# Output projection of a hybrid attention/gMLP layer from normalised inputs: one PSUM accumulation per piece, with a shorter 1/sqrt and other ends

## The chip, the cores and the metric

The kernel runs on one core of a Trainium2 chip. The metric is the device time of one execution in microseconds, taken as the median over runs. All arithmetic is float32 in effect: each operand of a large matrix product is split into a high and a low part of the narrower type fp32r, and three matmuls (high by high, low by high, high by low) stand for one product.

## The reference

One layer on 1056 tokens of width 1024 (1024 prompt tokens and 8 samples of 4 tokens). Cut to what matters here:

```python
x = x + 0.5 * swiglu(rmsnorm(x, ffn1_norm))           # FFN 1, width 2816
h = rmsnorm(x, mix_norm) @ w_in                       # q, k, v, u, g
attn = sink_attention(q, k, v)                        # 512 channels, window 128
gate = gelu(u) * (tril(w_s) @ rmsnorm(gelu(g)) + b)   # 512 channels, chunks of 128
x = x + concat(rmsnorm(attn, attn_out_norm),
               rmsnorm(gate, gmlp_out_norm)) @ w_out  # the output projection
x = x + 0.5 * swiglu(rmsnorm(x, ffn2_norm))           # FFN 2
y = rmsnorm(x, final_norm)
```

The output projection contracts over 1024 channels: 512 from the attention ("which = 0") and 512 from the gate ("which = 1"). Each half has a normalisation of its own, so each has a factor r per token, 1/sqrt(mean square), and a gain per channel.

## The kernel before, in words

Tokens lie in the free dimension, channels in the 128 partitions. The tokens are worked in two halves h = 0, 1 of 528, and a half in two pieces of 264, so that a piece fits one PSUM bank. Stages follow each other: FFN 1 (to about 700 us), the mixer (about 700 to 1080 us), FFN 2 and the final norm. A tile framework schedules each engine's instructions ahead of time; on the chip every engine runs its own queue in order, and waits at its head.

**Mixer.** A list of jobs sets the order: 28 jobs of the input projection (`proj`, 48 matmuls each, PSUM tile `pp`), then 16 of the output projection (`out_proj`, tile `pw`). The attention blocks (scores `sc` L860, exponentials on ACT L869, the sink's exponential L871, division L876, transposes `ptr` L883, product `po` L889) and the gate's pieces (`spatial`: transposes `pt` L788, squares L814, norm `gn` L819, mix `pm` L835 to L841) are generators that an interleaver `I` lets in between the matmuls of the jobs, at a rate per stage. Each job's weight, 128x1024, is loaded, cast on ACT (`whi` L114) and its remainder is taken by DVE or POOL (`wlo` L115). The weight of the next job is asked for when a job begins.

**Output projection.** `split_out` waits until a half's raw outputs are there, applies the gain and splits (`ah` ACT L972, `al` DVE L973). `out_proj` makes, for each output block d of 128 channels, each piece and each of the two contraction halves apart, 12 matmuls into a bank of its own. DVE multiplies the bank by r (`wo` L984), POOL adds the product to the residual x (L986). r comes from `norm_out` and `rstd`: squares summed over channel tiles (`oacc` L176), a sum over partitions by matmul (`pn` L150), 1/sqrt by integer guess and three Newton steps of three DVE operations on 128x5 elements (`tiny_rsqrt` L136 to L141, tiles `gt`, `gr`, `gv`), and a broadcast by matmul (`pr` L165). After the second half of the contraction, `final` splits x for FFN 2 (`xh` ACT L193, `xl` DVE L194), adds its squares (`acc` L176, on POOL for h = 0) and stores x.

**Start.** Ten warm-up matmuls, then x and the first weight block arrive by DMA; ACT casts two quarters of the weight (`wb` L121) and then makes the first operand (`xh` L193).

**End.** The last output piece of FFN 2 (`pd` L620, added to x on DVE L572) gets its square on ACT (L172), the square is added to the sum on DVE (`facc` L176), `pn` sums over partitions, DVE makes 1/sqrt, `pr` broadcasts it, ACT copies it (L1085), DVE and POOL scale the eight channel tiles (L1092, L1090), and the result is stored.

Of the kernel before, what the change touches and what calls it, by code (L numbers as in the profile page):

```python
# [11 lines left out]
F32 = mybir.dt.float32  # L12
# [28 lines left out]
def build(nc, tc, ctx, A):  # L41
# [91 lines left out]
    def tiny_rsqrt(a, n):  # L133

        b, c = small("gr", 5)[:, :n], small("gt", 5)[:, :n]
        V.tensor_scalar(c.bitcast(I32), a.bitcast(I32), 1, None, op0=ALU.arith_shift_right)  # L136
        V.tensor_scalar(b.bitcast(I32), c.bitcast(I32), -1, 0x5F3759DF, op0=ALU.mult, op1=ALU.add)
        for i in range(3):
            V.tensor_mul(c, b, b)
            V.scalar_tensor_tensor(c, c, -0.5, a, op0=ALU.mult, op1=ALU.mult)  # L140
            V.scalar_tensor_tensor(a if i == 2 else b, c, 1.5, b, op0=ALU.add, op1=ALU.mult)  # L141

    def rstd(acc, o, n, mul, eps, put):

        full, rest = n // 128, n % 128
        nj = full + (rest > 0)
        p = pst("pn")
        for j in range(nj):
            m = min(128, n - j * 128)
            PE.matmul(p[:m, j:j + 1], lhsT=acc[:, o + j * 128:o + j * 128 + m], rhs=ones[:, 0:1], start=True, stop=True)  # L150
        v = small("gv", 5)
        if rest:
            V.memset(v, 1.0)
            V.tensor_scalar(v[:rest, full:nj], p[:rest, full:nj], mul, eps, op0=ALU.mult, op1=ALU.add)
        V.tensor_scalar(v[:, :full], p[:, :full], mul, eps, op0=ALU.mult, op1=ALU.add)
        tiny_rsqrt(v[:, :nj], nj)
        yield 0.3, LAT["rstd"]

        p = pst("pr")
        for j in range(nj):  # L160
            m = min(128, n - j * 128)
            if j == 4:
                put(p, o)
                p = pst("pr2")
            PE.matmul(p[:, j % 4 * 128:j % 4 * 128 + m], lhsT=v[:m, j:j + 1].to_broadcast([m, 128]), rhs=ident[:m, :m], start=True, stop=True)  # L165
        put(p[:, :n] if nj <= 4 else p[:, :rest], o if nj <= 4 else o + 512)
        yield 1.0, 1
# [475 lines left out]
    pw = pst("warm")  # L643
    for _ in range(10):
        PE.matmul(pw[:, :128], lhsT=ones, rhs=ones, start=True, stop=True)
# [3 lines left out]
    for k in range(4):  # L649
        P1.split(0, k)  # L650
# [193 lines left out]
    def attention(b):  # L844
# [102 lines left out]
    parts, done = [[None, None], [None, None]], set()  # L947
    orst, held = [[None, None], [None, None]], []
# [4 lines left out]
    def norm_out(h, which):  # L953
        src, _ = raw_out(h, which)
        n = T[h]
        acc, r = tmp("oacc"), tmp("orst")
        orst[h][which] = r
# [4 lines left out]
        done.add((h, which))  # L962

    def split_out(h, which):
        I.until(lambda: finished.get((h, which)) is True)
        src, g0 = raw_out(h, which)
        n = T[h]
        hi, lo = Quad(f"ah{which}", 4, F32R), Quad(f"al{which}", 4, F32R)
        parts[h][which] = hi, lo
        for k in range(4):  # L970
            x, g = src(k, 0, n), gains[:, g0 + k:g0 + k + 1]
            S.activation(hi(k, 0, n), x, AF.Copy, scale=g)  # L972
            V.scalar_tensor_tensor(lo(k, 0, n), x, g, hi(k, 0, n).bitcast(F32), op0=ALU.mult, op1=ALU.subtract)  # L973

    def out_proj(h, which, i, w, prep, rate):
        hi, lo = parts[h][which]
        for d in (2 * i, 2 * i + 1):
            for hh, o, n in HPIECES[h]:
                p = pst("pw")
                mm3(p, n, w, hi, lo, range(4), o, lambda k: (4 * (d % 2) + k) * 128)  # L980

                def evac(d=d, o=o, n=n, p=p):
                    t = tmp("wo")
                    V.tensor_mul(t[:, :n], p[:, :n], orst[h][which][:, o:o + n])  # L984
                    x = X[h](d, o, n)
                    G.tensor_add(x, x, t[:, :n])  # L986
                    if which == 0 and (h, o, n) == HPIECES[h][-1]:
                        prep(h, d)
                held.append(evac)
                I(n * 12 / 2400, rate)  # L990
                if len(held) > 4:
                    I.until(lambda: (h, which) in done)
                if (h, which) in done:
                    while held:
                        held.pop(0)()
# [24 lines left out]
    jobs = [("p", h, kind, i) for h in range(2) for kind, i in kinds] + [("o", h, which, i) for h in range(2) for which in (1, 0) for i in range(4)]  # L1020
# [8 lines left out]
    def weight(t, h, kind, i):  # L1029
        return wload(A["w_in"][{"k": 0, "v": 1, "q": 2, "u": 6, "g": 10}[kind] + i] if t == "p" else A["w_out"][kind, i], lo_on=G if t == "p" and i else None)  # L1030

    w = weight(*jobs[0])
    wnext = weight(*jobs[1])
    for k in range(8):
        Pm.square(1, k)
    for job, ahead in zip(jobs, jobs[1:] + [None]):
        if job != jobs[0]:
            wnext = weight(*ahead) if ahead else None
# [35 lines left out]
    def one(piece, h, o, n, d):  # L1074
# [3 lines left out]
        squares(fin[piece], X[h](d, o, n), 0, n, first, V if piece else G)  # L1078
# [18 lines left out]
        ends.append(rstd(fin[piece], 0, n, 1.0 / D, 1e-6, put))  # L1097
# [39 lines left out]
def layout(i):  # L1137
# [11 lines left out]
    a["w_out"] = np.concatenate([w[:512][hd], w[512:]]).reshape(2, 4, 128, 4, 2, 128).transpose(0, 3, 2, 4, 1, 5).reshape(2, 4, 128, 1024)  # L1149
# [51 lines left out]
```

## Time and profile before

| | |
|---|---|
| time, three runs | 1785.37, 1787.62, 1787.37 us; median 1787.37 us |
| profiled execution | 1785.29 us, of which the span is 1783.5 us |
| TensorE busy | 1741.6 us of the span |
| VectorE busy | 1221.6 us |
| ScalarE busy | 730.9 us |
| GpSimd busy | 158.4 us |
| mean granted TensorE clock | 0.989 of full |

PE is TensorE's matmul, DVE is VectorE, ACT ScalarE, POOL GpSimd; L984 is line 984 of the kernel. A row of the timeline gives start, duration, engine, line, operation, output and inputs, and in square brackets how long the engine had been idle before and which engine's instruction ended that. A row of groups gives the total and the mean of one, and the idle time before them. Matmuls are pipelined: a 128x264 matmul is shown with a duration of 0.28 us, but the next one starts about 0.12 us later.

### The profile page before, as it was taken

Reading aid. Unit: us, or ns where it says so; the run is one execution under the profiler, and the core shown is the slowest. Engines: PE = TensorE matmul, PEld = TensorE weight load, DVE = VectorE, ACT = ScalarE, POOL = GpSimd, SP = SyncE. Lnnn points to the kernel's source line nnn. Section 1 sums busy time; section 2 is a strip of 40 time slices with the busy share of each in tenths; the row PEclk is TensorE's granted clock in tenths of the full one; section 3 lists DMA queues with packets and bytes.
Section 4 is the critical chain, followed back from the end, with each engine's and each line's share of the span. In section 5 each row is a group of like instructions: output and inputs, shape, how many; then the busy total and the mean of one; then the engine's idle time right before and its main releaser. Section 6 shows DMA issues by size and latency. Waiting matters only on the chain.

```text
span 1783.5 us, 34092 instructions
## 1 busy us (share of the span) xinstructions
PE 1741.6 (98%) x14045; PEld 1713.3 (96%) x14045; DVE 1221.6 (68%) x2151; ACT 730.9 (41%) x1288; POOL 158.4 (9%) x140
## 2 busy tenths in 40 slices
PE   9999999999999999999997899999999999999997
PEld 9999999999999999988977899999999999999997
DVE  7986766666556755488677886986666666457566
ACT  6533333333343444255464434633333333344341
POOL 0000000000000011221211571000000000000110
PEclk9999999999999999999998999999999999999998
DMA  6054544454495544112222232254544454586532
GB/s 240 28 190 160 201 157 150 145 201 150 153 378 169 166 135 140 67 49 75 72 72 65 101 102 85 67 206 149 195 153 140 172 182 138 209 327 200 175 107 98
DMA packets 104460, 266.05 MB, mean 149 GB/s; under 512 B 12384, under 2 KB 15136, under 8 KB 104288
## 3 DMA queue, kind: packets, MB, share of 16 engines
q1 hardware_dynamic: 104304, 263.87, 43.1%
q8 instruction: 110, 1.80, 0.4%
q14 instruction: 46, 0.38, 0.1%
HBM read 190.25 MB, written 74.60 MB: 148 GB/s over the span
## 4 chain that ended last, share of the span: by engine, by line
PE 79%; DVE 11%; issue 6%; POOL 2%; ACT 2%; DMA 0%; POOLq 0%; SPq 0%; DVEq 0%; ACTq 0%
PE pa L430 24%; PE pd L620 22%; PE pc L430 12%; PE pp L130 7%; PE pb L430 6%; PE pg L396 4%; PE pw L130 2%; POOL x L986 2%; DVE tl L299 1%; DVE wb L122 1%; ACT P L869 1%; DVE P L876 1%; DVE P L865 1%; PE po L889 1%; DVE raw L269 1%
## 5 line engine op out<-in xcount | busy, mean ns | idle before, releaser
L430 PE MATMUL pa<-th,wb 128*128 128x264 f32 x2624 | 494.7, 285 | 1.1 <-DVE wb L122 0.6
L430 PEld LDWEIGHTS pa<-th,wb 128*128 128x128 f32 x2624 | 413.1, 189 | 2.3 <-DVE wb L122 0.9
L430 PE MATMUL pa<-tl,wb 128*128 128x264 f32 x1312 | 374.3, 285 | 2.9 <-DVE tl L299 2.9
L620 PE MATMUL pd<-hh,whi 128*128 128x264 f32 x1208 | 343.9, 285 | 0.0
L620 PE MATMUL pd<-hl,whi 128*128 128x264 f32 x1208 | 343.8, 285 | 0.0
L620 PE MATMUL pd<-hh,wlo 128*128 128x264 f32 x1208 | 343.8, 285 | 0.0
L121 ACT CAST wb<-raw 128x512 fp32r<-128x512 f32 x296 | 181.3, 620 | 279.2 <-PE pc L430 83.4
L122 DVE TENSOR_TENSOR wb<-raw,wb 128x512 fp32r<-128x512 f32 x296 | 204.4, 700 | 107.1 <-ACT wb L121 106.5
L430 PEld LDWEIGHTS pa<-tl,wb 128*128 128x128 f32 x1312 | 247.6, 189 | 3.3 <-DVE tl L299 3.3
L430 PE MATMUL pc<-th,wb 128*128 128x264 f32 x1280 | 247.4, 285 | 1.4 <-DVE x L468 0.9
L620 PEld LDWEIGHTS pd<-hh,wlo 128*128 128x128 f32 x1208 | 227.6, 188 | 0.0
L620 PEld LDWEIGHTS pd<-hh,whi 128*128 128x128 f32 x1208 | 227.5, 188 | 0.1
L620 PEld LDWEIGHTS pd<-hl,whi 128*128 128x128 f32 x1208 | 227.3, 188 | 0.0
L430 PEld LDWEIGHTS pc<-th,wb 128*128 128x128 f32 x1280 | 204.0, 189 | 2.1 <-DVE x L468 1.1
L367 DVE TENSOR_TENSOR wlo<-raw,whi 128x1024 fp32r<-128x1024 f32 x82 | 94.8, 1156 | 134.7 <-ACT whi L366 125.9
L430 PE MATMUL pc<-tl,wb 128*128 128x264 f32 x640 | 182.6, 285 | 0.0
L269 DVE TENSOR_TENSOR raw<-raw 128x512 f32<-128x512 f32 x248 | 169.3, 691 | 16.0 <-DMA raw<-f_d 11.1
L366 ACT CAST whi<-raw 128x1024 fp32r<-128x1024 f32 x82 | 79.9, 980 | 216.1 <-PE pd L620 146.6
L130 PE MATMUL pp<-xh,wlo 128*128 128x264 f32 x448 | 129.3, 289 | 4.0 <-POOL wlo L115 4.0
L130 PE MATMUL pp<-xh,whi 128*128 128x264 f32 x448 | 131.7, 294 | 0.7 <-ACT whi L114 0.3
L130 PE MATMUL pp<-xl,whi 128*128 128x264 f32 x448 | 128.5, 287 | 0.0
L430 PEld LDWEIGHTS pc<-tl,wb 128*128 128x128 f32 x640 | 120.5, 188 | 0.3 <-DVE tl L299 0.3
(233 smaller groups left out, 3016.3 us busy)
## 6 DMA issues: line engine op xcount, KB each, us to landing
raw<-f_gu SPq DMA_DIRECT2D x86, 512.0 KB, 4.2
raw<-f_d SPq DMA_DIRECT2D x74, 512.0 KB, 3.9
ws_s<-raw SPq DMA_DIRECT2D x88, 256.0 KB, 2.0
ht<-ht_s SPq DMA_DIRECT2D x40, 528.0 KB, 7.6
raw<-ws_s SPq DMA_DIRECT2D x40, 512.0 KB, 8.4
raw<-w_in SPq DMA_DIRECT2D x28, 512.0 KB, 4.3
ht_s<-m SPq DMA_DIRECT2D x44, 264.0 KB, 2.2
ht<-ht SPq DMA_DIRECT2D x20, 528.0 KB, 3.8
```

The lines of the kernel that those rows point to most:

```text
L121: S.copy(w[:, 0], src)
L122: V.tensor_sub(w[:, 1], src, w[:, 0].bitcast(F32))
L130: PE.matmul(p[:, :n], lhsT=w[a][:, c:c + 128], rhs=b(k, o, n), start=(3 * i + j == 0), stop=(3 * i + j == last))
L269: V.tensor_add(b[dst], b[dst], b[x])
L299: V.tensor_sub(lo, src[kk], hi.bitcast(F32))
L366: S.copy(wh[:, :n * 512], raw[:, :n * 512])
L367: V.tensor_sub(wl[:, :n * 512], raw[:, :n * 512], wh[:, :n * 512].bitcast(F32))
L396: PE.matmul(p[:, :PC], lhsT=wk[:, a, c:c + 128], rhs=b[h](k, j * PC, PC), start=(k == 0 and i == 0), stop=(k == 7 and i == 2))
L430: PE.matmul(ps_[:, j], lhsT=w[:, a, kk * 128:(kk + 1) * 128], rhs=b[kk // 2][c][:, kk % 2, j * PC:(j + 1) * PC], start=(start and kk == 0 ...
L620: PE.matmul(ps_[d][:, j], lhsT=w[:, k * 512 + d * 128:k * 512 + (d + 1) * 128], rhs=t[:, k, j * PC:(j + 1) * PC], start=(bi == 0 and oi == ...
L865: V.tensor_tensor_reduce(Pt[c][:, g, :nk], s[c][:, i * 256:i * 256 + nk], alibi[:, hd, 256 - nk:], 1.0, sinks[:, hd:hd + 1], ALU.add, ALU. ...
L986: G.tensor_add(x, x, t[:, :n])
```

## The change

- `split_out` multiplies the raw outputs by gain and by r in place (DVE), copies the high part (ACT `oh`) and subtracts (DVE `ol`). It now waits until r is known. The matmuls therefore work on normalised operands, and `out_proj` accumulates the gate's 12 and the attention's 12 matmuls of a piece in one bank; one DVE add (L1004) adds the bank to x. There are 32 such adds; the 64 multiplications and the 64 POOL additions are gone. The weight is laid out by output block d, one load per d and half.
- `final` adds all squares on DVE; for h = 0 the split for FFN 2 is moved out of it, into the loop over h = 1.
- A job's weight is asked for two jobs ahead (`ahead(3)`) instead of one.
- `tiny_rsqrt` uses a cubic last step: seven operations after the guess instead of nine.
- In attention, the sink's exponential stands ahead of the eight large ones.
- Start: twelve warm-up matmuls; the first x tile's split stands ahead of the weight casts, and the second pair of weight quarters is fetched ahead of the third and fourth x tile.
- End: the last square isn't added on DVE; a second group of `pn` matmuls adds it in PSUM (`rstd(..., last)`), with warm-up matmuls between and behind (`busy`).

The order of TensorE where the output projection begins (`pw` is a bank; `ah1`/`al1` are the gate's operands for h = 0; `pm` is the gate's mix for h = 1). Before:

```order
L130 MATMUL pw_10989<-ah10_10977,whi_10803 128x264
...
L130 MATMUL pw_11005<-ah10_10977,whi_10803 128x264
...
L835 MATMUL pm_11018<-gate_c_7918,gn_10766 128x128 x4
L835 MATMUL pm_11026<-wts_7920,gns_10674 128x16
L130 MATMUL pw_11034<-ah10_10977,whi_10803 128x264
...
L130 MATMUL pw_11050<-ah10_10977,whi_10803 128x264
...
L130 MATMUL pw_11072<-ah10_10977,whi_10973 128x264
...
L788 MATMUL pt_11085<-ident_80,pv_10807 128x128 x4
```

The same place after (`oh_10791` is the gate's, `oh_10975` the attention's operand):

```order
L1001 MATMUL pw_10991<-oh_10791,whi_10592 128x264
...
L1001 MATMUL pw_11004<-oh_10791,whi_10592 128x264
...
L847 MATMUL pm_11017<-gate_c_7916,gn_10758 128x128 x4
L847 MATMUL pm_11025<-wts_7918,gns_10668 128x16
L1001 MATMUL pw_10991<-oh_10975,whi_10592 128x264
...
L1001 MATMUL pw_11030<-oh_10791,whi_10598 128x264
...
L1001 MATMUL pw_11004<-oh_10975,whi_10592 128x264
...
L1001 MATMUL pw_11030<-oh_10975,whi_10598 128x264
```

Each `pw` row opens a group of 12 matmuls. A bank is now returned to and closed after 24, and three banks are in work here where five separate ones were filled.

The order of TensorE where the two norms of h = 1 are broadcast (`pn` sums the squares, `pr` broadcasts r; the `oacc` are the sums of the attention's and the gate's squares). Before:

```order
L150 MATMUL pn_11595<-ones_78,oacc_11433 128x1 x4
L150 MATMUL pn_11595<-ones_78,oacc_11433 16x1
L130 MATMUL pw_11645<-ah00_11201,whi_11524 128x264
...
L165 MATMUL pr_11674<-ident_80,gv_11480 128x128 x4
L165 MATMUL pr2_11680<-ident_80,gv_11480 128x16
L130 MATMUL pw_11692<-ah00_11201,whi_11524 128x264
...
L165 MATMUL pr_11787<-ident_80,gv_11601 128x128 x4
L165 MATMUL pr2_11793<-ident_80,gv_11601 128x16
```

After:

```order
L160 MATMUL pn_11506<-ones_78,oacc_11385 128x1 x4
L160 MATMUL pn_11506<-ones_78,oacc_11385 16x1
L178 MATMUL pr_11531<-ident_80,gv_11416 128x128 x4
L178 MATMUL pr2_11537<-ident_80,gv_11416 128x16
L178 MATMUL pr_11540<-ident_80,gv_11512 128x128 x4
L178 MATMUL pr2_11546<-ident_80,gv_11512 128x16
L1001 MATMUL pw_11577<-oh_10791,whi_11355 128x264
```

The 24 and 60 projection matmuls that stood between the second `pn`, the first `pr` and the second `pr` stand behind both now. On VectorE the chain that the second `pr` waits for is mixed with other work there:

```order
L168 TENSOR_SCALAR gv_11512<-pn_11506 128x4
L136 TENSOR_SCALAR gt_11517<-gv_11512 128x5
L137 TENSOR_SCALAR gr_11516<-gt_11517 128x5
L115 TENSOR_TENSOR wlo_11574<-raw_11571,whi_11573 128x1024
L138 TENSOR_TENSOR gt_11517<-gr_11516 128x5
L189 TENSOR_TENSOR acc_11145<-acc_11145,sq_11527 128x528
L139 SCALAR_TENSOR_TENSOR gt_11517<-gt_11517,gv_11512 128x5
L985 SCALAR_TENSOR_TENSOR q0_9563<-q0_9563,gains_85,orst_11299 128x528
L140 SCALAR_TENSOR_TENSOR gr_11516<-gt_11517,gr_11516 128x5
L985 SCALAR_TENSOR_TENSOR q0_9563<-q0_9563,gains_85,orst_11299 128x528
L141 TENSOR_TENSOR gt_11517<-gr_11516 128x5
L985 SCALAR_TENSOR_TENSOR q1_9564<-q1_9564,gains_85,orst_11299 128x528
```

Two more 128x528 multiplications and three small operations follow ahead of `gv_11512`, on which the second `pr` waits.

The diff, cut to its core:

```diff
 tiny_rsqrt:
-        for i in range(3):
-            V.tensor_mul(c, b, b)
-            V.scalar_tensor_tensor(c, c, -0.5, a, op0=ALU.mult, op1=ALU.mult)
-            V.scalar_tensor_tensor(a if i == 2 else b, c, 1.5, b, op0=ALU.add, op1=ALU.mult)
+        V.tensor_mul(c, b, b)
+        V.scalar_tensor_tensor(c, c, -0.375 * 0.703952253, a, op0=ALU.mult, op1=ALU.mult)
+        V.scalar_tensor_tensor(b, c, 0.375 * 0.703952253 * 2.38924456, b, op0=ALU.add, op1=ALU.mult)
+        V.tensor_mul(c, b, b)
+        V.scalar_tensor_tensor(c, c, 1 / 0.375 ** 2, a, op0=ALU.mult, op1=ALU.mult)
+        V.scalar_tensor_tensor(c, c, -10.0 / 3.0, c, op0=ALU.add, op1=ALU.mult)
+        V.scalar_tensor_tensor(a, c, 5.0, b, op0=ALU.add, op1=ALU.mult)
+    def busy(n):
+        pw = pst("warm")
+        for _ in range(n):
+            PE.matmul(pw[:, :128], lhsT=ones, rhs=ones, start=True, stop=True)
 rstd(..., last=None):
+        terms = [acc] if last is None else [acc, last]
+        for t, a in enumerate(terms):
+            ...
+            if last is not None:
+                busy(7 if t else 4)
 start:
-    for _ in range(10):
-        PE.matmul(pw[:, :128], lhsT=ones, rhs=ones, start=True, stop=True)
+    busy(12)
+    P1.split(0, 0)
     load_x(0, 1, 2, 3)
     gb_.load(0, 3)
     gb_.plain("11", "21")
-    for k in range(4):
+    for k in range(1, 4):
         P1.split(0, k)
 attention:
+        V.tensor_add(mx, nm, sinks)
+        S.activation(mx, mx, AF.Exp)
         for hd in range(8):
             ...
-        V.tensor_add(mx, nm, sinks)
-        S.activation(mx, mx, AF.Exp)
 split_out:
-            S.activation(hi(k, 0, n), x, AF.Copy, scale=g)
-            V.scalar_tensor_tensor(lo(k, 0, n), x, g, hi(k, 0, n).bitcast(F32), op0=ALU.mult, op1=ALU.subtract)
+            V.scalar_tensor_tensor(x, x, gains[:, g0 + k:g0 + k + 1], r, op0=ALU.mult, op1=ALU.mult)
+            S.copy(hi, x)
+            V.tensor_sub(lo, x, hi.bitcast(F32))
 out_proj:
-                mm3(p, n, w, hi, lo, range(4), o, lambda k: (4 * (d % 2) + k) * 128)
-                    V.tensor_mul(t[:, :n], p[:, :n], orst[h][which][:, o:o + n])
-                    G.tensor_add(x, x, t[:, :n])
+        for which in (1, 0):
+            for d, w in zip(ds, ws):
+                for hh, o, n in HPIECES[h]:
+                    ...
+                    if not which:
+                        x = X[h](d, o, n)
+                        V.tensor_add(x, x, p[:, :n])
+                    I(n * 12 / 2400, rate)
+                if not which:
+                    final(h, d)
 final:
-        P2.split(h, d)
-        P2.square(h, d, V if h else G)
+        P2.square(h, d, V)
         load(spill[d, :, T0[h]:T0[h] + H], X[h](d, 0, H))
+        if h:
+            P2.split(1, d)
 job loop:
-            wnext = weight(*ahead) if ahead else None
+        ahead(3)
+        w = have.popleft()
+            if (h, kind, i) == (1, "g", 2):
+                split_out(0, 1)
+            if i == (0, 1):
+                split_out(h, 0)
+            out_proj(h, i, w, RATE[2 + h])
+            if h == 0 and i == (5,):
+                split_out(1, 1)
+            if h:
+                for d in i:
+                    P2.split(0, d)
 end:
-        squares(fin[piece], X[h](d, o, n), 0, n, first, V if piece else G)
+        end = None
+        if piece == 2 and d == 3:
+            end = tmp("sq")
+            S.activation(end[:, :n], X[h](d, o, n), AF.Square)
+        else:
+            squares(fin[piece], X[h](d, o, n), 0, n, first, V if piece else G)
```

More of the change, by code (lines that the diff above doesn't have):

```diff
@@ L147, in rstd @@
         p = pst("pn")
-        for j in range(nj):
-            m = min(128, n - j * 128)
-            PE.matmul(p[:m, j:j + 1], lhsT=acc[:, o + j * 128:o + j * 128 + m], rhs=ones[:, 0:1], start=True, stop=True)
+        terms = [acc] if last is None else [acc, last]
+        for t, a in enumerate(terms):
+            for j in range(nj):
+                m = min(128, n - j * 128)
+                PE.matmul(p[:m, j:j + 1], lhsT=a[:, o + j * 128:o + j * 128 + m], rhs=ones[:, 0:1], start=(t == 0 and (j == 0 or last is None)),
+                          stop=(t == len(terms) - 1), skip_group_check=last is not None)
+            if last is not None:
+                busy(7 if t else 4)
         v = small("gv", 5)
@@ L944, in sample_attention @@
         yield 0.8, 2
-    parts, done = [[None, None], [None, None]], set()
-    orst, held = [[None, None], [None, None]], []
+    OH, OL, factors = [None] * 2, [None] * 2, {}
     def raw_out(h, which):
@@ L956, in norm_out @@
         acc, r = tmp("oacc"), tmp("orst")
-        orst[h][which] = r
         for k in range(4):
@@ L970, in split_out @@
+        if OH[h] is None:
+            OH[h], OL[h] = [None] * 4, [None] * 4
         for k in range(4):
[L971 to L979, printed above, removed]
-                mm3(p, n, w, hi, lo, range(4), o, lambda k: (4 * (d % 2) + k) * 128)
[L982 to L995, printed above, removed]
@@ L1019, in build, with weights, ahead @@
     kinds = [("k", 0), ("v", 0)] + [(t, i) for t in "qug" for i in range(4)]
-    jobs = [("p", h, kind, i) for h in range(2) for kind, i in kinds] + [("o", h, which, i) for h in range(2) for which in (1, 0) for i in range(4)]
+    jobs = [("p", h, kind, i) for h in range(2) for kind, i in kinds] + [("o", h, None, ds) for h in range(2) for ds in ((0, 1), (2,), (3,), (4,), (5,), (6,), (7,))]
     spill = dram.tile([8, 128, NT], F32, name="spill")
     def final(h, d):
-        P2.split(h, d)
-        P2.square(h, d, V if h else G)
+        P2.square(h, d, V)
         load(spill[d, :, T0[h]:T0[h] + H], X[h](d, 0, H))
[L1029 to L1033, printed above, removed]
+        if h:
+            P2.split(1, d)
+    def weights(t, h, kind, i):
+        if t == "p":
+            return [wload(A["w_in"][{"k": 0, "v": 1, "q": 2, "u": 6, "g": 10}[kind] + i], lo_on=G if i else None)]
+        return [wload(A["w_out"][d]) for d in i]
+    todo, have = deque(jobs), deque()
+    def ahead(n):
+        while todo and sum(len(x) for x in have) < n:
+            have.append(weights(*todo.popleft()))
+    ahead(2)
     for k in range(8):
         Pm.square(1, k)
-    for job, ahead in zip(jobs, jobs[1:] + [None]):
-        if job != jobs[0]:
-            wnext = weight(*ahead) if ahead else None
+    for job in jobs:
+        ahead(3)
+        w = have.popleft()
         t, h, kind, i = job
@@ L1096, in one @@
             ends.pop()
-        ends.append(rstd(fin[piece], 0, n, 1.0 / D, 1e-6, put))
+        ends.append(rstd(fin[piece], 0, n, 1.0 / D, 1e-6, put, end))
     ffn(X, P2, A["f2_gu"], A["f2_d"], lambda i, h: pair(spill, i, T0[h], H), first, last, tail)
```

40 lines of the change are left out of this document (22 added, 18 removed).

## The prediction

> **What bounds the kernel now.** I read a table of windows by stage, then what TensorE waited for, and last the timeline at each wait. The windows' columns are the stretch, its length, then busy time and count of PE, PEld, DVE, ACT and POOL, the granted clock, the DMA share and GB/s.
>
> ```profile
> 0.00:60.00 60.00, 56.51 (x431) 55.74 (x432) 47.17 (x93) 38.46 (x69) 2.13 (x8) 0.97 0.49 179
> 60.00:700.00 640.00, 635.00 (x5184) 632.93 (x5183) 424.39 (x571) 246.45 (x353) 9.74 (x7) 1.00 0.51 174
> 700.00:900.00 200.00, 196.58 (x1572) 182.96 (x1571) 139.20 (x434) 100.51 (x275) 51.26 (x41) 1.00 0.20 64
> 900.00:940.00 40.00, 36.92 (x260) 32.42 (x262) 30.84 (x104) 24.09 (x79) 7.37 (x3) 0.91 0.25 80
> 940.00:1000.00 60.00, 50.83 (x369) 46.38 (x366) 46.58 (x139) 24.81 (x70) 17.30 (x18) 0.91 0.26 81
> 1000.00:1050.00 50.00, 45.15 (x349) 44.28 (x348) 42.69 (x83) 22.81 (x35) 35.20 (x31) 0.93 0.32 107
> 1050.00:1100.00 50.00, 48.39 (x396) 48.04 (x396) 37.53 (x60) 17.11 (x31) 22.55 (x23) 1.00 0.34 108
> 1100.00:1760.00 660.00, 659.59 (x5406) 658.66 (x5405) 443.07 (x640) 254.17 (x375) 10.74 (x7) 1.00 0.49 167
> 1760.00:1784.00 24.00, 12.59 (x94) 11.86 (x92) 10.09 (x33) 2.44 (x6) 2.14 (x3) 0.78 0.27 91
> ```
>
> TensorE sets the time: in FFN 2 it is busy 659.59 of 660 us, at 659.59 / 5406 = 0.122 us per matmul. The change leaves the number of projection matmuls as it is (64 groups of 12), so it can win only TensorE's idle time and what a lowered clock costs. Idle is window minus busy: 3.5 us at the start, 5.0 in FFN 1, 6.5 in the input projection up to 940, 9.2 + 4.85 + 1.6 = 15.6 in the output projection, 11.4 at the end. The clock is below full at the start, in 900 to 1050 and at the end.
>
> ```profile
> PE pr L165 <- DVE gv L141: 7.3, 3, 4.1
> PE pp L130 <- POOL wlo L115: 4.0, 2, 2.1
> ```
>
> The largest waits on compute, these two and the two in the next part, lie beside something that is edited.
>
> **The change part by part.** *The beginning of the output projection, 958 to 971.* Timeline of TensorE, ScalarE and VectorE:
>
> ```profile
> 958.07 0.59 PE L130 MATMUL pw<-ah,whi 128*128 128x264 f32 x1 [3.67 <-DVE mix L839]
> 960.66 0.42 PE L130 MATMUL pw<-ah,wlo 128*128 128x264 f32 x1
> 966.54 0.56 PE L130 MATMUL pw<-ah,whi 128*128 128x264 f32 x1 [5.46 <-DVE gn L819]
> 971.05 0.36 PE L130 MATMUL pw<-ah,whi 128*128 128x264 f32 x1
> 961.12 1.04 ACT L114 CAST whi<-raw 128x1024 fp32r<-128x1024 f32 x1 [3.71 <-PE pw L130]
> 965.27 1.12 DVE L819 TENSOR_SCALAR gn<-pt,gss 128x128 f32<-128x128 f32 x4
> ```
>
> This is a convoy. TensorE waits for a bank, so it ends its job late; ACT has a cast at its head that needs that job's weight buffer (3.71 us); behind the cast stand the gate's squares, behind those DVE's 1/sqrt and `gn`, and TensorE again waits for the bank that `gn` releases. Idle 3.67 + 5.46 = 9.13 us. Between 958.07 and 960.66 11 steps take 2.59 us, 0.235 each against 0.122, so 1.25 us is lost; 966.54 to 971.05 is as slow, and of its 4.51 us nearly half is lost, 2.1. Together 12.5.
>
> After, the second half of the contraction runs in the same banks, so three banks do what five did; the cast stands a job earlier; and TensorE has 54 independent matmuls (6.6 us) behind the `pm` group, of which only the attention's must wait for an `oh`. The evacuations of the first banks (32 adds in all) stand ahead of the gate's 1/sqrt on DVE. Following both queues by the durations of before I find a wait of 0 to 1.5 us and perhaps one short lapse of the clock left. I take **-10.0**, bounds -12.5 and -4 (the second wait, 5.46 and its slow steps, kept, the first gone with half of its price).
>
> *DVE's and POOL's load there.* Groups, 940 to 1100:
>
> ```profile
> L984 DVE TENSOR_TENSOR wo<-pw,orst 128x264 f32<-128x264 f32 x64 | 25.4, 422 | 2.8 <-PE pw L130 2.6 <-POOL x L986 0.2
> L194 DVE SCALAR_TENSOR_TENSOR xl<-x,gains,xh 128x528 fp32r<-128x528 f32 x16 | 12.3, 768 | 11.7 <-ACT xh L193 11.6
> L973 DVE SCALAR_TENSOR_TENSOR al<-q,gains,ah 128x528 fp32r<-128x528 f32 x6 | 5.6, 948 | 0.3 <-ACT ah L972 0.3
> L176 DVE TENSOR_TENSOR acc<-acc,sq 128x528 f32<-128x528 f32 x7 | 4.9, 702 | 0.0
> L973 DVE SCALAR_TENSOR_TENSOR al<-u,gains,ah 128x528 fp32r<-128x528 f32 x4 | 4.2, 1040 | 0.0
> L986 POOL TENSOR_TENSOR x<-x,wo 128x264 f32<-128x264 f32 x64 | 66.0, 1056 | 79.6 <-DVE wo L984 73.5 <-DVE gt L140 3.0 <-DVE gr L137 2.1
> ```
>
> Out go 25.4 and 5.6 + 4.2; in come 32 adds of 0.42 (13.5), for h = 1 eight multiplications of 0.768 and eight subtractions of 0.702 (11.8), and 4.9 of squares that POOL had. DVE had 46.58 + 42.69 + 37.53 = 126.8 of these 160 us; it loses 5. POOL's 66.0 us go, and with them whatever waited for them, off TensorE's path by itself. DVE is hardly cheaper; the gain comes from the order. But in the loop over h = 1 a block d costs DVE two adds, two splits, one square sum and a weight remainder, about 0.84 + 1.54 + 0.70 + 1.21 (the row of 1.21 is below), plus a share of FFN 2's first weights, 5.2 to 5.7 us against TensorE's 48 x 0.122 = 5.9. That is close; FFN 2 begins with DVE full. I charge **+1.0**, bounds 0 and +4.
>
> *The two norms of h = 1, 1012 to 1029.*
>
> ```profile
> 1024.29 0.98 PE L165 MATMUL pr<-ident,gv 128*128 128x128 f32 x3 [4.13 <-DVE gv L141]
> 1015.22 1.31 DVE L140 SCALAR_TENSOR_TENSOR gt<-gt,gv 128x5 f32<-128x5 f32 x1
> 1028.94 0.42 PE L130 MATMUL pw<-ah,whi 128*128 128x264 f32 x1
> 1019.15 1.21 DVE L115 TENSOR_TENSOR wlo<-raw,whi 128x1024 fp32r<-128x1024 f32 x1
> ```
>
> TensorE waited 4.13 us for a chain in which a step on 128x5 elements took 1.31 us (0.16 for the like at the end of the program, below) where a POOL addition ran beside it. All TensorE's rows from 1024.29 to 1028.94 are slow; of these 4.65 us nearly half is lost, 2.2: 6.3 in all. After, POOL is silent, but both broadcasts stand right behind the second `pn`, and the chain in front of the second one carries a remainder of 1.16 to 1.21, a sum of 0.70 and four multiplications of 0.77 beside nine small operations of 0.16: 1.2 + 0.7 + 3.1 + 1.4 = 6.4 us, some 5.9 of it idle TensorE, and again about 2 us of low clock. So 7.9 against 6.3: **+1.5**, bounds -2 and +4. Here the change gives back.
>
> *The weight asked for two jobs ahead.* TensorE, VectorE and POOL at 911:
>
> ```profile
> 914.00 0.59 PE L130 MATMUL pp<-xh,wlo 128*128 128x264 f32 x1 [2.11 <-POOL wlo L115]
> 919.67 0.42 PE L130 MATMUL pp<-xh,whi 128*128 128x264 f32 x1
> 911.39 6.40 DVE L876 TENSOR_SCALAR P<-P,den 128x256 f32<-128x256 f32 x8
> 911.46 4.86 POOL L115 TENSOR_TENSOR wlo<-raw,whi 128x1024 fp32r<-128x1024 f32 x2 [24.48 <-ACT whi L114]
> ```
>
> The cast stands behind eight exponentials, TensorE loses 2.11 us, and then 26 steps take 5.67 us (914.00 to 919.67) where 26 x 0.122 = 3.2 would do, 2.5 more: 4.6. The other such wait (at 794, the rest of the 4.0: 1.9) has no slow steps. With the earlier cast both go. But what is late next is the attention chain: DVE's divisions of the two blocks (6.40 us here while POOL works beside them, which it still does) feed transposes at 927 that TensorE would now reach at 922, and wait for. I take **-1.0** at 911 (bounds -4.6 and 0) and **-1.0** at 794 (-1.9 and 0, since DVE is nearly full behind it). The 1.6 of idle in 1050 to 1100 is one wait at 1081 on a `wo` that DVE reaches late, behind splits of x that follow POOL's additions: **-0.8** (-1.6 and 0).
>
> *Start.*
>
> ```profile
> 5.61 0.62 ACT L121 CAST wb<-raw 128x512 fp32r<-128x512 f32 x1 [0.73 <-DMA raw<-f_gu]
> 4.23 0.64 ACT L172 ACTIVATE acc<-x 128x528 f32<-128x528 f32 x1 [2.15 <-DMA x<-x]
> 7.88 0.76 PE L396 MATMUL pg<-xh,wb 128*128 128x264 f32 x4 [2.32 <-ACT xh L193]
> ```
>
> x's first tile was there at 4.23, where ACT squares it, so `xh` can run ahead of the cast and TensorE begin near 6.4, 1.5 us earlier. Later x tiles now arrive behind two more weight quarters, so some comes back: **-1.0** (-2 and +0.5). The two operations fewer of each 1/sqrt, 0.2 us each by the rows of the end below, count in FFN 1 only where a chain on DVE holds TensorE; I take one of its two chains, **-0.4** (-0.8 and 0).
>
> *End.*
>
> ```profile
> 1771.13 0.43 DVE L176 TENSOR_TENSOR facc<-facc,sq 128x264 f32<-128x264 f32 x1 [0.49 <-ACT sq L172]
> 1771.71 0.70 PE L150 MATMUL pn<-ones,facc 128*128 128x1 f32 x6 [1.54 <-DVE facc L176]
> 1772.90 0.17 DVE L137 TENSOR_SCALAR gr<-gt 128x3 int32<-128x3 int32 x1
> 1773.10 0.16 DVE L139 TENSOR_TENSOR gt<-gr 128x3 f32<-128x3 f32 x1
> 1774.98 1.71 PE L165 MATMUL pr<-ident,gv 128*128 128x128 f32 x6 [2.57 <-DVE gv L141]
> 1761.02 0.92 PE L165 MATMUL pr<-ident,gv 128*128 128x128 f32 x6
> ```
>
> The addition (0.43 and its step, 0.47) leaves the chain, though warm matmuls ahead of the second `pn` may take it back: -0.1. Two steps of 0.20 (1773.10 - 1772.90): -0.4. The six `pr` took 1.71 here and 0.92 at full clock; warm matmuls during the 2.57 idle keep it: -0.8. Sum **-1.3** (-1.8 and -0.6).
>
> A rule speaks against that last 0.8. The Trainium skill, "TensorE: Matmul & The Clock Gate", Part 1 (The HAM clock gate), says that the clock halves after an idle window of about 3.4 us. By that rule pauses of 2.57 or 2.11 us need not lower it, the warm matmuls would bring nothing and the sum would be 0.8 smaller; the rows above (1.71 against 0.92, and 0.42 after 2.11 us) show a lowered clock, so I go by them.
>
> *Sum:* -10.0 + 1.0 + 1.5 - 1.0 - 1.0 - 0.8 - 1.0 - 0.4 - 1.3 = -13.0 us against the profiled execution's 1785.29 us, 1772.3. That execution lies 2.1 below the median of the runs, so **1774.4** is what a median should show. All bounds at once give -27.2 and +3.9.
>
> **The rivals.** *The stall only moves* (A). Half of the gain at 958 comes back, because what starves TensorE there is the attention chain on ACT and DVE, which no edit shortens. For it: the transposes at 927. Against: DVE had 46.58 of 60 us in 940 to 1000, not full. The sum loses 5 to 7: 1780.
>
> *Everything goes* (B). The chain at 927 isn't late, because the divisions run beside a silent POOL: 911 gives 4.6 and 958 all of 12.5, 6.1 more: 1768.
>
> *Slower* (C). One mechanism: the split of h = 1 now needs r before its first matmul, and the multiplications stand on DVE inside the chain for r. If the convoy at 958 keeps its 5.46 us wait and slow steps (-4 instead of -10) and DVE takes over 0.122 x 48 = 5.9 us per block d, TensorE waits in each of eight blocks. It decides from about 7 us per block: 8 x 1.1 = 9, and the two norms at their bound add 2.5: -13 + 6 + 9 + 2.5 = +4.5, 1792. For it: 5.7 against 5.9 is close and DVE is full behind. Against: POOL, which stretched DVE's small operations, is silent.
>
> *Nothing* (D). The waits in the middle change places and cancel, start and end give 2.7 less 1: 1786.
>
> **How the numbers follow.** Mine has 0.55, A 0.17, B 0.13, C 0.07, D 0.08. The range 1765 to 1786 leaves out C and the far parts of B. What a measurement can tell is about 0.2%, 3.6 us, so faster means under 1783.8: mine, B and most of A, 0.83. D and the rest of A are the same, 0.10. C is slower, 0.07.
>
> **What would show it right or wrong.** Right: TensorE's idle time in 940 to 1000 falls from 9.2 to under 3 with the clock above 0.95; one wait of 5 to 7 us at the `pr` L178 near 1010 to 1020 with a lowered clock behind it; no row "pp <- POOL wlo"; the six `pr` at the end at 0.9 us; the first `pg` before 6.6 us. Wrong: an ACT cast in 950 to 970 that waits over 3 us for TensorE (A or C), waits for an add L1004 in each block after 1030 (C), or no wait at the transposes near 925 (B).

## The result and the profile after

The changed kernel takes 1773.56 us (median of four runs, 1772.4 to 1774.72) against 1786.92 us before (four runs), a ratio of 0.993 with a 95% interval of 0.9918 to 0.9941. The forecast was 1774.4, 1765 to 1786. The profiled execution took 1773.43 us, 1771.7 of it the span.

The windows of the changed kernel, with the columns as before; the last stages are moved to where they lie now:

```profile
0.00:60.00 60.00, 57.30 (x444) 56.06 (x445) 47.82 (x90) 39.47 (x70) 1.84 (x8) 1.00 0.49 179
60.00:700.00 640.00, 635.08 (x5178) 632.99 (x5177) 424.06 (x570) 245.65 (x353) 9.73 (x7) 1.00 0.51 174
700.00:900.00 200.00, 195.26 (x1546) 181.50 (x1546) 137.63 (x416) 98.05 (x267) 51.01 (x42) 0.99 0.20 63
900.00:940.00 40.00, 35.48 (x252) 31.74 (x252) 31.89 (x97) 24.95 (x78) 7.61 (x3) 0.87 0.22 74
940.00:1000.00 60.00, 59.96 (x463) 53.96 (x463) 49.63 (x156) 30.97 (x86) 0.00 (x0) 1.00 0.35 117
1000.00:1050.00 50.00, 45.58 (x347) 44.91 (x348) 35.52 (x75) 21.67 (x36) 0.00 (x0) 0.93 0.31 101
1050.00:1090.00 40.00, 40.00 (x331) 40.00 (x330) 20.98 (x36) 13.36 (x25) 0.00 (x0) 1.00 0.29 95
1090.00:1750.00 660.00, 659.63 (x5417) 658.71 (x5416) 442.36 (x635) 254.12 (x375) 10.74 (x7) 1.00 0.49 167
1750.00:1772.00 22.00, 14.27 (x117) 13.67 (x115) 9.17 (x29) 2.45 (x6) 2.15 (x3) 0.87 0.29 99
```

The 60 us from 940 on, which held 9.2 us of idle and a clock of 0.91, are full now: 59.96 busy at full clock. But 700 to 940 got worse, 4.7 + 4.5 us idle instead of 3.4 + 3.1, and the clock in 900 to 940 is 0.87. What TensorE waits for now:

```profile
PE pr L178 <- DVE gv L144: 7.3, 3, 4.4
PE pa L443 <- DVE tl L312: 2.8, 2, 2.5
PE pt L800 <- DVE pv L752: 2.7, 1, 2.7
PE spo L946 <- ACT spt L943: 1.5, 1, 1.5
PE ptr L895 <- ACT PT L896: 1.5, 3, 0.7
```

The remainder of POOL and the two banks of the convoy are gone from the list; new are `pt`, `spo` and `ptr`, all in the input projection.

A table by stage sets the two profiled executions beside each other and beside the terms of the sum. Each stage runs from one matmul to another, by their starts in the two timelines (`pg` opens each FFN, `pp` the input projection, `pw` the output projection):

| stretch | before | after | change | terms of the prediction |
|---|---|---|---|---|
| start to first `pg` | 7.88 | 6.62 | -1.3 | -1.0 |
| to first `pp` (FFN 1) | 696.93 | 697.96 | +1.0 | -0.4 |
| to first `pw` (input projection) | 243.42 | 248.91 | +5.5 | -2.0 |
| to the second `pn` of h = 1 | 58.03 | 45.42 | -12.6 | -10.0 |
| to last `pw` (the two norms, then h = 1) | 72.32 | 72.19 | -0.1 | +1.5 |
| to last `pd` (FFN 2) | 691.31 | 688.11 | -3.2 | +1.0 - 0.8 |
| to the end | 13.61 | 12.49 | -1.1 | -1.3 |
| sum | 1783.5 | 1771.7 | -11.8 | -13.0 |

In both traces the three middle stages hold the same matmuls (1850, 357 and 530 by start), so their lengths can be compared. The total is right, and the largest term too, but the input projection went the other way by 7.5 us, and the total came out because the convoy gave 2.6 more and FFN 2 3.4 more than I took. So the open question was what the input projection lost. TensorE's idle time in that stage grew from 6.5 to 9.3 us, and the mean granted clock fell from 0.99 to 0.97.

Its places, in the changed kernel. First the broadcast of the first norm at 711 to 720, on VectorE, POOL and TensorE:

```profile
713.16 1.17 DVE L138 TENSOR_TENSOR gt<-gr 128x5 f32<-128x5 f32 x1
714.36 2.32 DVE L139 SCALAR_TENSOR_TENSOR gt<-gt,gv 128x5 f32<-128x5 f32 x1
716.72 2.28 DVE L140 SCALAR_TENSOR_TENSOR gr<-gt,gr 128x5 f32<-128x5 f32 x1
719.03 0.17 DVE L141 TENSOR_TENSOR gt<-gr 128x5 f32<-128x5 f32 x1
714.27 4.71 POOL L115 TENSOR_TENSOR wlo<-raw,whi 128x1024 fp32r<-128x1024 f32 x2
719.85 1.48 PE L178 MATMUL pr<-ident,gv 128*128 128x128 f32 x10 [2.27 <-DVE gv L144]
```

And the same place before, where TensorE waited 0.57 us:

```profile
714.61 2.31 DVE L140 SCALAR_TENSOR_TENSOR gt<-gt,gv 128x5 f32<-128x5 f32 x1
716.96 0.17 DVE L141 SCALAR_TENSOR_TENSOR gr<-gt,gr 128x5 f32<-128x5 f32 x1
714.51 2.39 POOL L115 TENSOR_TENSOR wlo<-raw,whi 128x1024 fp32r<-128x1024 f32 x1
```

A step of 0.17 us on 5 elements takes as long as the POOL operation beside it. The weight asked for two jobs ahead put a second remainder there (x2 instead of x1), and a second step was held. The Trainium skill, "SBUF — State Buffer" (Who interferes with whom), says that a VectorE instruction with two inputs in SBUF contends with a GpSimd instruction that reads SBUF, since its second input comes through a read interface that both share, and that the shared port pair is an exclusive lock. By these rows the trace agrees: the two steps took 2.32 and 2.28 us beside two POOL operations of 4.71 together.

Then 898 to 935:

```profile
898.87 3.81 POOL L115 TENSOR_TENSOR wlo<-raw,whi 128x1024 fp32r<-128x1024 f32 x1 [12.20 <-ACT whi L114]
900.34 2.62 DVE L752 SCALAR_TENSOR_TENSOR u<-gs,u 128x264 f32<-128x264 f32 x1
904.11 0.48 PE L946 MATMUL spo<-spt,VS 16*128 16x128 f32 x2 [1.50 <-ACT spt L943]
917.76 6.48 DVE L888 TENSOR_SCALAR P<-P,den 128x256 f32<-128x256 f32 x8
930.77 0.69 PE L800 MATMUL pt<-ident,pv 128*128 128x128 f32 x2 [2.74 <-DVE pv L752]
```

The operation of 0.43 us took 2.62, the eight divisions took 6.48, and TensorE waited behind both, the second time with the clock down. The second wait comes by a longer way: the next block's eight exponentials on ScalarE could only begin at 925.79, behind the divisions, and the gate's GELU step (L751), which `pv` and then `pt` wait for, stood behind them until 929.84. That the remainder no longer stops TensorE itself is true, and of no use while it stops VectorE.

### The profile page after: what moved, and what is told of

It is laid out like the page before. It is cut to its first block, busy times and chain, and to the rows that moved or that the text cites. A ratio compares the mean times of both kernels' runs of the same rounds, so it can differ in the third digit from the quotient of the medians.

```text
span 1771.7 us, 33954 instructions
## 1 busy us (share of the span) xinstructions
PE 1742.6 (98%) x14077; PEld 1713.5 (97%) x14077; DVE 1199.1 (68%) x2099; ACT 730.7 (41%) x1288; POOL 83.1 (5%) x69
## 4 chain that ended last, share of the span: by engine, by line
PE 86%; DVE 7%; issue 5%; ACT 2%; DMA 0%; SPq 0%; POOLq 0%; POOL 0%; DVEq 0%; ACTq 0%
PE pa L443 25%; PE pd L633 22%; PE pc L443 12%; PE pp L130 7%; PE pb L443 6%; PE pw L1001 5%; PE pg L409 4%; DVE tl L312 1%; DVE wb L122 1%; ACT P L883 1%; PE po L901 1%; DVE P L888 1%; PE pr L178 1%; PE pm L847 1%; DVE raw L282 1%
```

## The experiments

Theory 1 was that of the prediction: the gain is the convoy at the beginning of the output projection, resolved by the order of the work; the small edits are small. The rivals: that the convoy went because POOL's additions went; that the shared bank did it; and, for the input projection, that the earlier request, the seven-step 1/sqrt or the order of the exponentials did the harm, or POOL's remainders beside VectorE. All ratios below are to the kernel before, with 95% intervals; stretches come from one profiled execution each.

**The new output projection alone**: weights one job ahead, the sink's exponential last, Newton steps, start and end of before.

```diff
-        ahead(3)
+        ahead(2)
(and tiny_rsqrt, attention, start and end as in the kernel before)
```

> The new output projection alone: weights one job ahead, the sink's exponential last, three Newton steps, and the start and end of before. Theory 1 (the gain is the convoy at the beginning of the output projection, and the other edits add up to nearly nothing): TensorE idle in the 60 us that hold the first projection matmuls under 1 us, the whole near 1776, 10 to 12 us under before. Theory 2 (the weight fetched earlier and the cheaper chains keep ScalarE and VectorE free there): the convoy stays in part, an idle wait of 3 us or more before an output projection matmul, the whole 1780 to 1784.

Measured: 1774.57 us, 0.9932 (0.992 to 0.9945). That is as fast as the whole change within the intervals. From first `pw` to the second `pn` 47.6 us (58.0 before, 45.4 with the whole change), no wait above 0.78 us there, though 1.7 us of idle time in 940 to 1000, where I expected under 1: Theory 1. The input projection takes 246.1 us, 2.7 longer than before, with none of the small edits in the kernel. Eight multiplications for h = 0 stand in this stage, 7.2 us of VectorE, and I had counted only those of h = 1; that it is they that cost the 2.7 us wasn't tried alone.

**One job ahead.**

```diff
-        ahead(3)
+        ahead(2)
```

> The changed kernel with the weight asked for one job ahead, as before. If the earlier request is worth what the prediction took (2.0 us, two waits of TensorE for POOL's remainder gone and part of it lost at the next transposes): such waits of 1.9 and 2.1 us return and the time is 1775 to 1777. Rival (the earlier cast only moves POOL's remainder onto other VectorE work, so it brings nothing or harms): 1771 to 1774, and the first output projection matmul no later than in the changed kernel.

Measured: 1772.31 us, 0.9916 (0.9903 to 0.993): no slower, the rival. The waits for the remainder return (1.88 and 2.10 us), the wait at the broadcast near 718 falls from 2.27 to 0.18, and the first `pw` starts at 953.15 instead of 953.49. The rows at that broadcast show why: one remainder, one held step.

```profile
714.37 2.32 DVE L139 SCALAR_TENSOR_TENSOR gt<-gt,gv 128x5 f32<-128x5 f32 x1
716.72 0.17 DVE L140 SCALAR_TENSOR_TENSOR gr<-gt,gr 128x5 f32<-128x5 f32 x1
714.28 2.39 POOL L115 TENSOR_TENSOR wlo<-raw,whi 128x1024 fp32r<-128x1024 f32 x1
```

**Three Newton steps.**

```diff
-        (seven operations after the guess, and the guess's constant)
+        for i in range(3):
+            V.tensor_mul(c, b, b)
+            V.scalar_tensor_tensor(c, c, -0.5, a, op0=ALU.mult, op1=ALU.mult)
+            V.scalar_tensor_tensor(a if i == 2 else b, c, 1.5, b, op0=ALU.add, op1=ALU.mult)
```

> The changed kernel with three Newton steps (nine operations) in place of the seven. If fewer operations help wherever a chain holds TensorE: five or six places by 0.2 to 0.4 us, 1774.5 to 1775.5. Rival (in the chain at 711 to 720 what counts is how many small steps meet a POOL addition, and the seven met one more): the wait at the broadcast there falls from 2.27 back to about 0.6 us, and the whole stays within 1 us, 1772.5 to 1774.5.

Measured: 1776.12 us, 0.9937 (0.9925 to 0.995). The median lies above both expected ranges, and the interval overlaps that of the change; the trace is clearer. The wait at the broadcast near 720 is 2.67, not 0.6: the seven steps are not what lost there, and this rival falls. Input projection 250.9 (248.9 in the changed kernel), first to last `pw` 119.3 (117.6): by these two stretches two operations fewer are worth 3.6 us, by the medians 2.6, more than the 0.4 that I took outside the end; with overlapping intervals this is a hint and not a measured size.

**The sink's exponential last.**

```diff
-        V.tensor_add(mx, nm, sinks)
-        S.activation(mx, mx, AF.Exp)
         for hd in range(8):
             ...
+        V.tensor_add(mx, nm, sinks)
+        S.activation(mx, mx, AF.Exp)
```

> The changed kernel with the sink's exponential behind the eight large ones, as before. Prediction's view (it costs and brings nothing): 1773 to 1774. Rival (it shortens the chain from the last exponential to the divisions by 0.1 to 0.2 us in each of eight blocks, and TensorE waits for that in some): 1774 to 1775.

Measured: 1771.73 us, 0.9914 (0.99 to 0.9927), its span 1771.7 us like that of the changed kernel, the input projection 248.7 us against 248.9. The median lies 1.8 us under the changed kernel's, below both expected ranges, but the intervals overlap and the stages agree: no effect is shown.

**The gate's split of h = 1 one output block later.**

```diff
-            if h == 0 and i == (5,):
+            if h == 0 and i == (6,):
                 split_out(1, 1)
```

> The changed kernel with the gate's split of h = 1 asked for one output block later, so that the second of the two norms gets 24 projection matmuls ahead of each broadcast, and the split 48 instead of 96 matmuls of cover. If the wait of 4.42 us at the broadcast and the half clock behind it (about 2 us) are a matter of order alone: the wait under 1 us, a new one of 0 to 2 us at the first projection matmul of h = 1, the whole 1768 to 1771. Rival (the split needs all its cover): 4 us or more of wait at the first matmul of h = 1, the whole 1772 to 1775.

Measured: 1765.9 us, 0.9887 (0.9873 to 0.99), under the changed kernel's interval and 2 us under what I expected. In the changed kernel the wait and the slow matmuls behind it stand in these rows:

```profile
1005.82 2.61 PE L178 MATMUL pr<-ident,gv 128*128 128x128 f32 x10 [4.42 <-DVE gv L144]
1008.75 0.42 PE L1001 MATMUL pw<-ol,whi 128*128 128x264 f32 x1
1011.61 0.42 PE L1001 MATMUL pw<-oh,wlo 128*128 128x264 f32 x1
```

Here both broadcasts come without a wait and at full clock, and no wait appears at the first matmul of h = 1:

```profile
1001.84 1.37 PE L178 MATMUL pr<-ident,gv 128*128 128x128 f32 x10
1006.19 1.37 PE L178 MATMUL pr<-ident,gv 128*128 128x128 f32 x10
```

The stretch from the second `pn` to the last `pw` is 64.9 us instead of 72.2. So the give-back of the two norms was as the prediction told it, and a matter of order; 48 matmuls cover the split.

**Weight remainders on VectorE.**

```diff
-        return [wload(..., lo_on=G if i else None)]
+        return [wload(..., lo_on=None)]
```

> The changed kernel with the weight remainders of the input projection taken by VectorE instead of POOL (26 operations of about 1.16 us, 30 us more for VectorE in 240). If POOL's remainders, which run beside VectorE's small steps and divisions and stretch them, are what costs the input projection its 5.5 us: the wait at the broadcast near 720 falls from 2.27 to under 0.6 us, no division of eight longer than 3 us, the output projection starts 3 to 6 us earlier, the whole 1767 to 1771. Rival (VectorE is the engine that TensorE waits for there, stretched or not): the first output projection matmul no earlier, the whole 1774 to 1780.

Measured: 1758.79 us, 0.9848 (0.9834 to 0.9861): 14.8 us under the changed kernel, beyond what I expected. The input projection takes 235.0 us instead of 248.9. The two stages as windows, the changed kernel first, with the columns as before:

```profile
704.58:953.49 248.91, 239.65 (x1852) 218.61 (x1851) 178.40 (x557) 126.23 (x359) 57.23 (x43) 0.97 0.20 64
```

```profile
704.77:939.80 235.03, 232.83 (x1853) 214.09 (x1851) 173.25 (x575) 125.81 (x359) 15.03 (x25) 1.00 0.21 68
```

TensorE's idle time falls from 9.3 to 2.2 us, 7.1 of the 13.9; the rest is about what a clock of 0.97 instead of 1.00 costs in 249 us. POOL gives up 42 us of work, and VectorE, which takes it over, is itself busy 5 us less. Groups of the changed kernel, 704 to 953:

```profile
L888 DVE TENSOR_SCALAR P<-P,den 128x256 f32<-128x256 f32 x48 | 21.7, 525 | 0.0
L752 DVE SCALAR_TENSOR_TENSOR u<-gs,u 128x264 f32<-128x264 f32 x16 | 9.1, 566 | 1.9 <-ACT gs L751 1.8
L115 POOL TENSOR_TENSOR wlo<-raw,whi 128x1024 fp32r<-128x1024 f32 x18 | 45.5, 2533 | 159.4 <-ACT whi L114 108.5 <-DVE gss L824 35.8 <-DVE mx L877 15.2
```

The same stage of this kernel, 704 to 939:

```profile
L888 DVE TENSOR_SCALAR P<-P,den 128x256 f32<-128x256 f32 x48 | 13.1, 349 | 0.0
L752 DVE SCALAR_TENSOR_TENSOR u<-gs,u 128x264 f32<-128x264 f32 x16 | 6.9, 430 | 1.6 <-ACT gs L751 1.6
L115 DVE TENSOR_TENSOR wlo<-raw,whi 128x1024 fp32r<-128x1024 f32 x28 | 35.8, 1278 | 4.9 <-ACT whi L114 4.9
```

VectorE does 18 more remainders (I had counted 26) and a division still falls from 525 to 349 ns in the mean; the wait at the broadcast near 718 is gone, at `spo` too. The theory of POOL's remainders holds, its rival falls.

**Two banks.** Normalised operands, each half of the contraction in its own bank, 64 additions:

```diff
-                    if which:
-                        banks[d, o] = pst("pw")
-                    p = banks[d, o]
+                    p = pst("pw")
...
-                    if not which:
-                        x = X[h](d, o, n)
-                        V.tensor_add(x, x, p[:, :n])
+                    x = X[h](d, o, n)
+                    V.tensor_add(x, x, p[:, :n])
```

> The changed kernel, normalised operands as they are, but each half of the contraction in a bank of its own and added to the residual by itself: 64 additions on VectorE instead of 32, 13.5 us more. Theory 1 (the convoy went because nothing waits for POOL and the operands come early, not because of the shared bank): the 60 us from the first projection matmul on stay free of waits over 1 us, the whole 1773 to 1776. Theory 2 (holding fewer banks is what freed TensorE): a wait of 3 us or more for a bank returns there, the whole 1778 to 1785.

Measured: 1775.72 us, 0.9937 (0.9925 to 0.995); TensorE is busy 58.58 of the 60 us from 940 on, the longest wait 1.18. The shared bank is not what freed TensorE; the 13.5 us of VectorE that it saves are worth 2.2 us by the medians, with overlapping intervals.

**Start and end of before.**

```diff
-    busy(12)
-    P1.split(0, 0)
+    busy(10)
...
-        if piece == 2 and d == 3:
+        if False:
```

> The changed kernel with the start and the end of before. By the prediction's terms (1.0 and 1.3 us) it takes 1775 to 1776.5; the first product begins near 7.9 to 8.3 us instead of 6.6, and the stretch from the last output matmul to the end is 13.6 us instead of 12.5. Rival (the start's gain is lost in the first 700 us, since VectorE is full there): the first matmul of the mixer no later than in the changed kernel, the whole 1774 to 1775.

Measured: 1775.32 us, 0.9933 (0.992 to 0.9947); the interval overlaps the change's. First `pg` at 8.60 instead of 6.62, and the last stretch 13.4 us instead of 12.5; the mixer begins 1.6 us later (706.20 against 704.58). Both terms are there, at about the size I took (of my 1.3 us for the end, 0.4 are the shorter 1/sqrt, which this kernel keeps).

**The kernel before with its additions on VectorE.**

```diff
-                    G.tensor_add(x, x, t[:, :n])
+                    V.tensor_add(x, x, t[:, :n])
```

> The kernel before, with the 64 additions of the output projection on VectorE instead of POOL (27 us more for VectorE, nothing left on POOL there); the order of the halves, the held products and the splits stay. If the convoy at 958 to 966 came from POOL (its additions late, and its reads in the way of VectorE): the two waits of 3.67 and 5.46 us shrink to under 2 in all, the whole 1774 to 1779. Rival (the convoy is a matter of the order in which banks are filled and freed, and of ScalarE's cast waiting for TensorE): both waits stay within 1.5 us of what they were, the whole 1784 to 1792.

Measured: 1779.96 us, 0.9964 (0.9951 to 0.9976). It lies between the two expectations, but the convoy tells them apart. TensorE and ScalarE:

```profile
958.67 0.59 PE L130 MATMUL pw<-ah,whi 128*128 128x264 f32 x1 [2.65 <-DVE mix L839]
967.15 0.56 PE L130 MATMUL pw<-ah,whi 128*128 128x264 f32 x1 [5.47 <-DVE gn L819]
```

```profile
961.71 1.04 ACT L114 CAST whi<-raw 128x1024 fp32r<-128x1024 f32 x1 [3.71 <-PE pw L130]
```

Both waits stand, 2.65 and 5.47 us where they were 3.67 and 5.46, and the cast's 3.71 us to the hundredth. POOL's additions were not the cause. What this kernel gains comes later: the wait of 4.13 at the broadcast is gone, though one of 2.27 for a `wo` is new.

**The kernel before with its remainders on VectorE.**

```diff
-lo_on=G if t == "p" and i else None
+lo_on=None
```

> The kernel before, with the weight remainders of the input projection on VectorE instead of POOL. If POOL's remainders beside VectorE cost the input projection as much as in the changed kernel (where moving them gave 14.8 us): 1770 to 1777, no wait of TensorE for a remainder, the division of 6.40 us back at 2.2. Rival (the request two jobs ahead is needed to make it pay, since with one job ahead TensorE stands behind cast and remainder): waits of TensorE for the remainder of 1 us and more, now on VectorE, the whole 1780 to 1787.

Measured: 1781.01 us, 0.9964 (0.9951 to 0.9978). That is the rival's range, and its waits are there: the input projection is 3.5 us shorter and a division is at 346 ns, but TensorE waits 1.64, 1.53 and 1.61 us for cast or remainder, asked for one job ahead. The convoy stays here too, with waits of 2.92 and 5.46 us, so POOL's remainders didn't make it either.

**Both improvements, weights two jobs ahead, and one job ahead.**

```diff
-            if h == 0 and i == (5,):
+            if h == 0 and i == (6,):
-        return [wload(..., lo_on=G if i else None)]
+        return [wload(..., lo_on=None)]
(second kernel also: ahead(2))
```

> The changed kernel with both: remainders on VectorE, and the gate's split one output block later, weights two jobs ahead. If the two gains add (14.8 and 7.7 us): 1750.5 to 1752.5. Rival (each takes part of the same slack, since the split's cover is VectorE time): 1753 to 1757.

> The same with weights one job ahead. If the earlier request brings nothing by itself even without POOL: 1750.5 to 1753, as the one before within 1 us. If it pays once the remainder no longer disturbs VectorE: 1753 to 1758, with waits of TensorE for the cast or the remainder in the input projection.

Measured: 1753.97 us, 0.9817 (0.9803 to 0.983), with two jobs ahead; 1757.28 us, 0.9835 (0.9821 to 0.9848), with one. The first is the fastest kernel of this study, 33 us under before, with a mean clock of 0.998; 22.5 us were expected of the two if they add, 19.6 found, which is the rival's range. By the stages its reason doesn't hold: the input projection takes 234.9 us (235.0 with the remainders alone), and from the second `pn` to the last `pw` it is 64.9 (64.9 with the later split alone), so neither gain eats into the other where it arises. In the profiled spans the two add to within 0.7 us (13.0 and 7.3 against 19.6); the medians' further 2 us are as much as the runs of either kernel differ among themselves. The earlier request seems to pay once no remainder disturbs VectorE: with one job ahead TensorE waits again, in the input projection:

```profile
793.71 0.39 PE L130 MATMUL pp<-xh,wlo 128*128 128x264 f32 x1 [1.62 <-DVE wlo L115]
826.74 0.39 PE L130 MATMUL pp<-xh,whi 128*128 128x264 f32 x1 [0.80 <-ACT whi L114]
829.78 0.39 PE L130 MATMUL pp<-xh,wlo 128*128 128x264 f32 x1 [1.49 <-DVE wlo L115]
```

The whole intervals of the two overlap; the four runs of each, 1753.8 to 1754.5 and 1756.7 to 1758.0 us, and the input projections, 234.9 and 238.6 us, don't leave much doubt.

## Why the prediction was right, and where not

- **What bounds the kernel**: right. TensorE's work is the same, and all of the change is in waits and the clock.
- **The convoy, -10.0**: right, a little small. The measured -12.6 is the whole 12.5 that I had counted, with nothing of the residue of 0 to 1.5 us. What resolved it isn't POOL (the convoy stays with the additions on VectorE, and with the remainders there), nor the bank (it stays away with two), nor the earlier request (it stays away with one job ahead). What is left, by elimination, is the order: two blocks at once and the casts for them placed earlier, with operands that need no factor behind the matmul. No run tests the order by itself, nor which of its parts is enough.
- **VectorE's load, +1.0**: not seen in the loop over h = 1, where TensorE is busy all of 1050 to 1090. The entry to FFN 2 went well: from first to last `pg` 49.0 us instead of 50.9, the wait of 1.6 gone (-0.8 taken). The rest of FFN 2, 1.3 us shorter, I leave unexplained: from its last `pg` to its last `pd` the kernels of this study took 638.96 to 641.01 us.
- **The two norms, +1.5**: the mechanism was right, wait and low clock both, and order was the cure. The wait was 4.42 where I had 5.9. Without wait and low clock the stretch takes 64.9 us, so they cost 7.3 in the changed kernel, near my 7.9; but the kernel before, at 72.3, had already lost 7.4 there, where I had counted 6.3, and so the stretch came out even.
- **The weight two jobs ahead, -1.0 and -1.0**: this step failed. I wrote that the waits go, which they did, and that the attention chain would be late next, and bounded the term at nothing lost. Instead the second remainder fell on the 1/sqrt at 711 (+1.7), and the earlier remainders still fell on VectorE's chain; with one job ahead the stage takes 248.6 us, with two 248.9, so the request brought nothing. I had the row that says so (6.40 us for eight divisions beside POOL), used it for a bound, and didn't ask where the moved remainder would land. Beside it I left out the eight multiplications of h = 0: the new projection alone made this stage 2.7 us longer. That and the request's 0.3 are not all of the 5.5. The other 2.5 us came with the small edits together, and undoing one of them alone leaves 250.9 us (1/sqrt), 248.7 (exponential) or 247.6 (start and end), so their source stays open; what the runs show is that the loss goes when POOL has no remainder.
- **Start, 1/sqrt and end**: start and end about as taken (the first `pa` comes at 60.9 instead of 61.9 us). The shorter 1/sqrt, taken at 0.4 in FFN 1, shows nothing there (697.8 us with three Newton steps, 698.0 with seven operations); the 2.6 by the medians lie nearly all in the mixer. FFN 1 took 1.0 more, where I took 0.4 less, and that stays open; from first `pa` to its last the kernels take either 414.1 to 414.5 or 415.4 to 416.0 us, and the last section shows what decides it.
- **The rivals**: none came out whole. B's half at 958 did, its half at 911 didn't. A's reason, an attention chain that is late near 927, was there, but in the input projection, and TensorE waited for it at the gate's transposes `pt` (2.74 us) and not at the attention's `ptr`. Of the signs that would show my forecast right two missed in size: the wait at `pr` was under 5 us, and the first `pg` came at 6.62.

So the total was right partly by luck: the convoy and FFN 2 gave 6 us more than I took and the two norms 1.6 more, and the input projection 7.5 less.

## What to carry to other kernels

When a prefetch is moved earlier, count every operation that it issues on every engine and look at what runs there at the new place: here the remainder left TensorE's path and landed on VectorE's 1/sqrt, and nothing was won. An operation on POOL that runs beside VectorE isn't free: here 18 remainders of 2.5 us on POOL cost more than the same work in about 1.28 us each on VectorE. And two sums that a broadcast waits for belong ahead of independent matmuls, not right ahead of their use.

## What the runs showed of the hardware

The same pause lowers the clock in one run and not in another. At one place in FFN 1, near 110 us, TensorE waits 2.43 to 2.46 us in all fourteen profiled executions. In ten of them the granted clock then falls to half; in four it doesn't (the new output projection alone, the gate's split one block later, the kernel before with its additions on VectorE, and both improvements with one job ahead). From the first `pa` to the last the ten take 415.4 to 416.0 us and the four 414.1 to 414.5. The changed kernel, and behind it the one with the gate's split later, each with 3.41 us behind the pause:

```profile
110.53 0.39 PE L443 MATMUL pa<-tl,wb 128*128 128x264 f32 x1 [2.46 <-DVE tl L312]
110.92:114.33 3.41, 3.41 (x18) 3.41 (x17) 3.25 (x6) 0.00 (x0) 0.00 (x0) 0.50 0.89 317
```

```profile
110.91 0.39 PE L443 MATMUL pa<-tl,wb 128*128 128x264 f32 x1 [2.46 <-DVE tl L312]
110.92:114.33 3.41, 3.41 (x28) 3.41 (x29) 3.41 (x6) 1.05 (x3) 0.00 (x0) 1.00 0.74 239
```

The first matmul behind the pause takes 0.39 us in both, so it doesn't tell the two apart; the clock falls a little later, and then 18 matmuls stand where 28 do at full clock. 3.41 us at half clock lose 1.7, so a pause of about 2.5 us may cost 1.7 us more or nothing, and an estimate should hold both ends. The free-running window of the Trainium skill, "TensorE: Matmul & The Clock Gate", Part 1 (The HAM clock gate), would explain why it depends on the moment; its 3.4 us of idle as what it takes does not fit, since 2.46 us were enough. And warm-up matmuls in a pause do keep the clock: the six broadcasts at the end took 0.99 or 1.00 us in all nine kernels that have them, and 1.71 or 1.72 in the five that don't, among them the changed kernel with the end of before, after a pause of 2.18 us.

```profile
1763.91 0.99 PE L178 MATMUL pr<-ident,gv 128*128 128x128 f32 x6 [0.64 <-DVE gv L144]
```
